# The state space model's input in DRAM: stored gapless and once, instead of with a repeated strip

## The chip, the cores and the metric

The kernel runs on 1 core of one Trainium2 chip. The metric is the device time of one execution in microseconds (us), median of several runs.

## What is computed

Two layers of a diffusion backbone over 768 tokens (256 context tokens, then 512 latent tokens), width 1024. In each layer four groups of heads share one input projection and one output projection: a complex diagonal state space model (S5), a Hyena long convolution, a retention, and a latent attention; then comes a gated feed-forward network. The change touches the S5 group alone:

```python
uc, ul = groups(u_ctx), groups(u_lat)
hc_f = s5_scan(uc, abar[0], bbar[0], None)
hc_b = s5_scan(uc[:, ::-1], abar[1], bbar[1], None)
hl_f = s5_scan(ul, abar[0], bbar[0], hc_f[:, -1])
hl_b = s5_scan(ul[:, ::-1], abar[1], bbar[1], hc_b[:, -1])
...
y = y.reshape(bsz, n, W_GROUP) + d_skip.astype(f32) * u.astype(f32)
y = jax.nn.gelu(y)
y = y * jax.nn.sigmoid(y @ glu_w.astype(f32) + glu_b.astype(f32))
```

The forward scan runs over context, then latent tokens. The backward scan runs over the context reversed, then over the latent tokens reversed; this is the same as reading the order "latent, context" from its end.

## The kernel before, in words

The input projection (L341 and L356, three fp32r passes a product) runs job after job on TensorE (PE). Weights come through `load_w` (L301: a DMA of 512 KB into one of three buffers `wr`; L305: a cast to `wh` on ScalarE (ACT); L306: the rest `wl` on VectorE (DVE)). Beside the projection jobs run generators, a few steps after each job: `chain_a` (S5 and retention), `chain_b` (attention, with its heads' scores at L1360 to L1362 and exponentials at L1420), `chain_h` (Hyena). In layer 0 retention comes before S5 in `chain_a`, in layer 1 S5 comes first. Each engine runs its instructions in one fixed order; an instruction that waits holds up all behind it on its engine.

The S5 group takes 8 neighbouring tokens as one chunk: NCH = 96 chunks, of which 32 are context and 64 latent. A channel's row is stored as [j = 8 tokens of a chunk][n = chunk].

- `s5_in` (L965 to L974) runs twice a layer, once for each 128 channels. ACT copies the projection from PSUM into a tile `t` [128, 8, 96] (L970, L971). Two DMAs on SP's queue store it into `s5_u`, whose rows are [8, 128]: L973 stores all 96 chunks of each j (runs of 384 bytes), L974 stores chunks 0 to 31 once more behind them, at 96 to 127 (runs of 128 bytes), so that a row reads context, latent, context.
- `s5_run` (from L976) turns the data: tile U (tag A_U) holds (j, channel in group) on the partitions and (group, chunk) along a row. For each j one DMA on POOL's software queue (L983) loads 16 partitions x 16 groups x 128 chunks: 256 runs of 512 bytes, 128 KB. Between them L984 loads the matching part of the matrix T (tag A_T), also 128 KB, 512-byte runs. `states` (L1001) multiplies U[.., 0:96] for the forward direction and U[.., 127:31:-1] for the backward one. `outputs` (L1033 to L1041) writes y, ACT's queue stores it to `s5_y` (L1050).
- At the end, the skip term d_skip * u needs u once more in its first layout: L1067 reads it from `s5_u` on SP's queue, as 8 runs of 384 bytes a channel in layer 0, and of 256 bytes (latent chunks alone) in layer 1. L1068 reads y, L1069 adds them on DVE, L1070 is the gelu.

Queues around the change: SP issues all weight loads and nearly all other transfers; POOL issues U, T and the four row copies of each pair of attention heads (L1371, L1373); ACT issues `s5_y`. POOL also computes the reciprocal roots of the norms (L404) and clears a column of the scan tiles (L1017).

Of the kernel before, what the change touches and what calls it, by code (L numbers as in the profile page):

```python
# [19 lines left out]
L = 2  # L20
# [7 lines left out]
NCH = NT // 8  # L28
# [197 lines left out]
def tile_kernel(ctx, tc, I, out, dbg=None, upto=None):  # L226
    nc = tc.nc
    act, dve, pe, pool, sp = nc.scalar, nc.vector, nc.tensor, nc.gpsimd, nc.sync
    qa, qs, qv, qb, qy, qh, qc, qm, qw, qp = [dict(s=sp, a=act, p=pool)[c] for c in QUEUES]
# [6 lines left out]
    def new(p, shape, tag, dt=F32, **kw):  # L236
        return p.tile(list(shape), dt, tag=tag, name=nm(tag), **kw)
# [22 lines left out]
    def st_tile(dt=F32):  # L260
        return new(wp, [128, NT], "st", dt, bufs=4)
# [167 lines left out]
    def dtile(shape, tag):  # L429
        return new(dr, shape, tag)  # L430
# [5 lines left out]
    s5_rot = [dtile([2, 4, 128, 576], f"s5_rot{l}") for l in range(L)]  # L436
    hy_K = [dtile([4, 2, 128, 768], f"hy_K{l}") for l in range(L)]
    hy_Kc = dtile([2, 2, 128, 768], "hy_Kc")
    s5_u = [dtile([256, 8, 128], f"s5_u{l}") for l in range(L)]
    s5_y = [dtile([256, 8, NCH], f"s5_y{l}") for l in range(L)]  # L440
    cat_d = [[dtile([128, NT], f"cat{l}_{i}") for i in range(8)] for l in range(L)]
    pd = [[dtile([128, NT], f"pd{l}_{i}") for i in range(19)] for l in range(L)]
# [522 lines left out]
    def s5_in(l, inproj):  # L965
        for i in range(2):
            o = inproj(i, (1, 0), True)
            t = st_tile().rearrange("p (j n) -> p j n", j=8)
            tv = t.rearrange("p j n -> p n j")
            act.copy(tv[:, 32:96], o[1].rearrange("p (n j) -> p n j", j=8))  # L970
            act.copy(tv[:, 0:32], o[0].rearrange("p (n j) -> p n j", j=8))  # L971
            u = s5_u[l][128 * i:128 * i + 128]
            qs.dma_start(u[:, :, 0:96], t)  # L973
            qs.dma_start(u[:, :, 96:128], t[:, :, 0:32])  # L974

    def s5_run(l, p, put, segs, busy=lambda: False):  # L976
        ud, yd = s5_u[l].rearrange("(g c) j n -> j c g n", c=16), s5_y[l].rearrange("(g c) j n -> j c g n", c=16)
        n0 = 0 if 0 in segs else 32
        nn = NCH - n0
        U = new(p, [128, 16, 128], "A_U")  # L980
        T = new(p, [128, 16, 128], "A_T")
        for j in range(8):
            qp.dma_start(U[16 * j:16 * j + 16], ud[j])  # L983
            qp.dma_start(T[16 * j:16 * j + 16].rearrange("c g (i x) -> c g i x", i=8), s5_T[l][:, :, j:j + 8, :])  # L984
        tt = dve.tensor_tensor

# [77 lines left out]
        for i in range(2):  # L1064
            tu = new(p, [128, 2, 8, NCH], ("A_U", "A_T")[i])
            t, u = tu[:, 0], tu[:, 1]
            qc.dma_start(u[:, :, n0:], s5_u[l][128 * i:128 * i + 128][:, :, n0:96])  # L1067
            qc.dma_start(t[:, :, n0:], s5_y[l][128 * i:128 * i + 128][:, :, n0:])  # L1068
            dve.scalar_tensor_tensor(t[:, :, n0:], u[:, :, n0:], vec256[:, l, 0, i:i + 1], t[:, :, n0:], ALU.mult, ALU.add)  # L1069
            act.activation(t[:, :, n0:], t[:, :, n0:], AF.Gelu_apprx_tanh)  # L1070
            yr.append(t)
            un.append(u.rearrange("p j n -> p (j n)"))
# [548 lines left out]
    for l in range(L):  # L1621
# [4 lines left out]
        def inproj(i, sg, fine=False):  # L1626
            if i in opened:
                return opened.pop(i).rest()
            return dense(blk(load_w(fl(I["w_in"][l, i]))), of(H), range(KD), sg, fine)
# [40 lines left out]
        with ExitStack() as base, ExitStack() as esl, ExitStack() as esr:  # L1670
# [5 lines left out]
            if l == 0:  # L1676
# [9 lines left out]
                with mkpool("start", side="right") as px:  # L1686
# [30 lines left out]
                    sp.dma_start(rr, I["k_rrope"])  # L1717
                    lgam = ret_gamma(px)
            s5_in(l, inproj)

            def ip_hyena(i):
# [52 lines left out]
            def chain_a(p):  # L1774
                for c in ORDER[l]:
                    if c == "s":
                        yield from s5_run(l, p, put, segs)
                    else:
                        while not (have("r") and have("g")):
                            yield  # L1780
                        yield from ret(l, p, put, segs)
                while spec or not have("h"):
                    yield
                if l == 0:
                    yield from hyena(l, p, put, 0, dict(v="A_U", x1=None, o="A_CA", y="A_SB", ny=2, kt="A_GT", u="A_HS", ri=None, pr=None))
# [73 lines left out]
        if True:  # L1859
# [47 lines left out]
            with mkpool("F") as p:  # L1907
# [38 lines left out]
                for gi, gn in enumerate(FFG):  # L1946
                    mid = []
                    for t in range(t0, t0 + gn):
                        uv = []
                        for w in range(2):  # L1950
                            run(g, W_FF)
                            o = product(("up", 2 * t + w), fl(I["w_up"][l, 2 * t + w]), H, segs)
                            u = st_tile()
# [65 lines left out]
def _build(nc, arrays, dbg=None, upto=None):  # L2019
    I = {k: nc.dram_tensor("in_" + k, v.shape, mybir.dt.from_np(v.dtype), kind="ExternalInput").ap() for k, v in arrays.items()}  # L2020
    out = nc.dram_tensor("out_x", [128, KD, NL], F32, kind="ExternalOutput").ap()
    with tile.TileContext(nc, schedule_with_timeline_sim=TLS) as tc:
        tile_kernel(tc, I, out, dbg, upto)
# [12 lines left out]
```

## Time and profile before

| | us |
|---|---|
| median of 3 runs | 2082.46 |
| lowest, highest | 2080.05, 2084.06 |
| the profiled execution, its own time | 2080.39 |
| its span, first to last instruction | 2078.6 |

The profile is of one execution. Times are us from the span's start. In a timeline row stand: start, duration, engine, line, operation, tile written and tile read, count, and in brackets the idle time before it with what ended it. A suffix q (SPq, ACTq) means the engine's sequencer, where DMAs are issued. In a row by windows stand: the stretch, its length, then for PE, PE's weight loads, DVE, ACT and POOL the busy time and (in brackets) the instructions, then the clock granted to PE (1.00 is 2.4 GHz, 0.50 is 1.2 GHz), the mean busy share of the 16 DMA engines (a little over 1 where packets of several queues overlap) and GB/s. In a row of waits stand: the engine and line that waited, for whom, us in total, times, longest. In a row of DMA queues stand: packets, MB, and the time of their packets as a share of 16 engines in that stretch; in one of DMA issues the transfer, the queue, the count, its size, and median us from issue to landing.

### The profile page before, as it was taken

How to read it: one execution, taken by the hardware profiler on the slowest of the kernel's cores; microseconds unless marked ns; L12 is line 12 of the kernel's file. 1: busy time of each engine (PE TensorE's matmuls, PEld its weight loads, DVE VectorE, ACT ScalarE, POOL GpSimd, SP SyncE). 2: the span in 40 equal slices, each digit the busy share in tenths (PEclk: the TensorE clock that was granted, in tenths of full speed). 3: DMA queues.
4: the chain of work that ended last, by engine and by line, in shares of the span. 5: the costliest groups of instructions: out<-in, count | busy, mean ns of one | idle time of the engine just before them, and what ended most of it. 6: DMA issues, size and time to landing. Idle time of an engine off the chain costs nothing. (4 is left out here: it accounts for less than half of the span.)

```text
span 2078.6 us, 29481 instructions
## 1 busy us (share of the span) xinstructions
PE 1912.3 (92%) x11318; PEld 1559.5 (75%) x11318; DVE 1299.4 (63%) x2444; ACT 788.0 (38%) x1349; POOL 172.3 (8%) x195
## 2 busy tenths in 40 slices
PE   5998999787899799899999999889989989999997
PEld 1866766566788688788888888778857878888885
DVE  4767553686735997776765444739857445555554
ACT  4546322343234433333533233433255434333332
POOL 0221013100001000110000000110022010000001
PEclk8999999889999899999999999999989989999998
DMA  8556556635442568234234222486631324333331
GB/s 299 178 182 227 168 177 172 147 78 175 148 152 92 172 216 276 78 115 140 63 98 149 68 65 67 119 215 184 217 98 53 133 85 128 93 100 94 99 99 44
DMA packets 147125, 283.94 MB, mean 137 GB/s; under 512 B 35397, under 2 KB 78566, under 8 KB 146984
## 3 DMA queue, kind: packets, MB, share of 16 engines
q1 hardware_dynamic: 139304, 273.65, 41.5%
q0 software_dynamic: 3072, 7.08, 1.9%
q10 hardware_dynamic: 4608, 1.31, 0.3%
q8 instruction: 90, 1.47, 0.3%
q14 instruction: 51, 0.42, 0.1%
HBM read 230.12 MB, written 48.99 MB: 134 GB/s over the span
## 5 line engine op out<-in xcount | busy, mean ns | idle before, releaser
L306 DVE TENSOR_TENSOR wl<-wr,wh 128x1024 fp32r<-128x1024 f32 x174 | 213.9, 1231 | 285.3 <-ACT wh L305 285.1
L341 PE MATMUL mm<-H1h,wh 128*128 128x512 f32 x888 | 355.6, 400 | 14.1 <-DVE st L426 13.1
L341 PE MATMUL mm<-H1h,wl 128*128 128x512 f32 x888 | 353.2, 398 | 0.3 <-DVE wl L306 0.3
L341 PE MATMUL mm<-H1l,wh 128*128 128x512 f32 x888 | 352.9, 397 | 0.0
L305 ACT CAST wh<-wr 128x1024 fp32r<-128x1024 f32 x174 | 182.1, 1050 | 356.7 <-PE mm L341 299.8
L341 PEld LDWEIGHTS mm<-H1h,wh 128*128 128x128 f32 x888 | 168.5, 190 | 55.3 <-issue 13.2
L341 PEld LDWEIGHTS mm<-H1l,wh 128*128 128x128 f32 x888 | 168.4, 190 | 38.8 <-issue 2.6
L341 PEld LDWEIGHTS mm<-H1h,wl 128*128 128x128 f32 x888 | 168.4, 190 | 37.8 <-issue 0.8
L341 PE MATMUL mm<-H0h,wh 128*128 128x256 f32 x480 | 137.0, 286 | 8.7 <-DVE st L426 8.5
L341 PE MATMUL mm<-ff_mh,wh 128*128 128x512 f32 (+1 forms) x432 | 134.9, 362 | 8.5 <-DVE y L1943 3.8
L341 PE MATMUL mm<-H0l,wh 128*128 128x256 f32 x480 | 137.5, 286 | 0.0
L341 PE MATMUL mm<-H0h,wl 128*128 128x256 f32 x480 | 137.4, 286 | 0.0
L341 PE MATMUL mm<-ff_ml,wh 128*128 128x512 f32 (+1 forms) x432 | 133.3, 359 | 0.0
L341 PE MATMUL mm<-ff_mh,wl 128*128 128x512 f32 (+1 forms) x432 | 132.7, 359 | 0.0
L404 POOL TENSOR_TENSOR rq_y<-rq_v,halves 128x2 f32<-128x2 f32 (+3 forms) x37 | 34.8, 942 | 1155.3 <-DVE rq_v L403 702.7
L341 PEld LDWEIGHTS mm<-H0h,wh 128*128 128x128 f32 x480 | 91.9, 191 | 12.8 <-issue 12.0
L341 PEld LDWEIGHTS mm<-H0l,wh 128*128 128x128 f32 x480 | 91.6, 191 | 5.3 <-issue 4.6
L341 PEld LDWEIGHTS mm<-H0h,wl 128*128 128x128 f32 x480 | 91.7, 191 | 4.0 <-issue 3.7
L341 PEld LDWEIGHTS mm<-ff_mh,wh 128*128 128x128 f32 x432 | 73.1, 191 | 24.0 <-DVE y L1943 5.3
L1943 DVE TENSOR_TENSOR y<-mm,y 128x512 f32<-128x512 f32 x80 | 53.4, 687 | 58.9 <-PE mm L341 58.8
L424 ACT ACTIVATE st<-mm,c_ffn_v 128x512 f32<-128x512 f32 (+1 forms) x132 | 88.3, 700 | 4.6 <-PE mm L356 4.6
L425 DVE SCALAR_TENSOR_TENSOR st<-mm,c_ffn_v,st 128x511 f32<-128x511 f32 (+1 forms) x132 | 83.4, 654 | 3.5 <-ACT st L424 3.5
(609 smaller groups left out, 4142.4 us busy)
## 6 DMA issues: line engine op xcount, KB each, us to landing
wr<-in_w_up SPq DMA_DIRECT2D x88, 512.0 KB, 3.6
ar<-in_ada_t SPq DMA_DIRECT2D x48, 512.0 KB, 4.4
wr<-in_w_down SPq DMA_DIRECT2D x44, 512.0 KB, 3.6
ar<-in_ada_w SPq DMA_DIRECT2D x40, 512.0 KB, 5.6
wr<-in_w_in SPq DMA_DIRECT2D x34, 512.0 KB, 5.7
ar<-in_k_tabl SPq DMA_DIRECT2D x16, 512.0 KB, 4.2
wr<-in_w_out SPq DMA_DIRECT2D x16, 512.0 KB, 4.9
xs_d<-x SPq DMA_DIRECT2D x8, 1024.0 KB, 4.7
```

The source lines that it names most:

```text
L305: act.copy(hi, raw)
L306: dve.tensor_tensor(lo, raw, hi.bitcast(F32), ALU.subtract)
L341: pe.matmul(outs[s], w, X(k, s, j), start=f, stop=z)
L404: pool.tensor_tensor(y, v, halves[:, :n], ALU.pow)
L424: act.activation(u[:, o:o + m], ps, AF.Identity, bias=vw[:, 3:4], scale=vw[:, 1:2])
L425: dve.scalar_tensor_tensor(u[:, o + 1:o + m], ps[:, 0:m - 1], vw[:, 0:1], u[:, o + 1:o + m], ALU.mult, ALU.add)
L1943: dve.tensor_tensor(d, ps, d, ALU.add)
```

## The change

`s5_u` gets rows of [8, 96], gapless. `s5_in` stores each tile with one DMA, whose runs are whole rows (8 x 96 x 4 = 3072 bytes). U is loaded by two DMAs for each j: chunks 0 to 95 (runs of 384 bytes) into columns 0 to 95, and chunks 0 to 31 once more (runs of 128 bytes, 32 KB) into columns 96 to 127. The skip term's read takes whole rows, in layer 1 the context chunks too. Instructions of a layer: SP issues 2 DMAs fewer, POOL 8 more.

```diff
-    s5_u = [dtile([256, 8, 128], f"s5_u{l}") for l in range(L)]
+    s5_u = [dtile([256, 8, NCH], f"s5_u{l}") for l in range(L)]
...
-            u = s5_u[l][128 * i:128 * i + 128]
-            qs.dma_start(u[:, :, 0:96], t)
-            qs.dma_start(u[:, :, 96:128], t[:, :, 0:32])
+            qs.dma_start(s5_u[l][128 * i:128 * i + 128], t)
...
-            qp.dma_start(U[16 * j:16 * j + 16], ud[j])
+            qp.dma_start(U[16 * j:16 * j + 16, :, 0:NCH], ud[j])
+            qp.dma_start(U[16 * j:16 * j + 16, :, NCH:128], ud[j][:, :, 0:128 - NCH])
             qp.dma_start(T[16 * j:16 * j + 16].rearrange("c g (i x) -> c g i x", i=8), s5_T[l][:, :, j:j + 8, :])
...
-            qc.dma_start(u[:, :, n0:], s5_u[l][128 * i:128 * i + 128][:, :, n0:96])
+            qc.dma_start(u, s5_u[l][128 * i:128 * i + 128])
```

## Rows read from the trace of the kernel before

**Rows 1.** The page's first part, busy time.
```profile
PE 1912.3 (92%) x11318; PEld 1559.5 (75%) x11318; DVE 1299.4 (63%) x2444; ACT 788.0 (38%) x1349; POOL 172.3 (8%) x195
```

**Rows 2.** Windows around S5's loads, layer 0 (375 on), layer 1 (1390 on).
```profile
375.00:380.00 5.00, 1.56 (x6) 0.97 (x6) 2.57 (x5) 0.84 (x3) 3.69 (x7) 0.76 1.14 224
380.00:385.00 5.00, 3.53 (x10) 2.98 (x11) 1.03 (x2) 0.93 (x2) 1.81 (x5) 0.50 1.05 124
...
1390.00:1400.00 10.00, 10.00 (x46) 8.68 (x46) 3.21 (x4) 4.34 (x8) 0.00 (x0) 0.76 0.67 222
```

**Rows 3.** Waits of PE, stretch 340 to 420 (first) and 1340 to 1400.
```profile
PE mm L1360 <- DMA B_Q<-st: 5.7, 2, 3.8
...
PE mm L341 <- DVE st L426: 8.5, 1, 8.5
```

**Rows 4.** Timeline of ACT, layer 1.
```profile
1385.78 1.04 ACT L305 CAST wh<-wr 128x1024 fp32r<-128x1024 f32 x1 [11.00 <-DMA wr<-in_w_v]
1386.73 0.77 ACT L424 ACTIVATE st<-mm,c_hy_v 128x512 f32<-128x512 f32 x1
```

**Rows 5.** Timeline of SP's DMA issues, layer 1.
```profile
1349.75 5.43 SPq L989 DMA_DIRECT2D A_SB<-s_SB  x1
...
1357.09 2.50 SPq L301 DMA_DIRECT2D wr<-in_w_in  x1
...
1367.96 0.99 SPq L301 DMA_DIRECT2D wr<-in_w_v  x2
```

**Rows 6.** Timeline of POOL, layer 1.
```profile
1362.25 1.12 POOL L983 DMA_DIRECT2D A_U<-s_u  x2 [16.16 <-DMA s_u<-st]
...
1370.43 0.56 POOL L984 DMA_DIRECT2D A_T<-s_T  x1 [3.75 <-DMA A_U<-s_u]
```

**Rows 7.** DMA queues, 1364 to 1388: the software queue and its landings.
```profile
q0 software_dynamic: 528, 1.44, 35.8%
...
wr<-in_w_v SPq DMA_DIRECT2D x2, 512.0 KB, 17.7
A_U<-s_u POOLq DMA_DIRECT2D x5, 128.0 KB, 13.0
```

**Rows 8.** Windows: the first store of s5_u (layer 0), and large runs alone (layer 1).
```profile
72.00:73.00 1.00, 1.00 (x10) 1.00 (x10) 1.00 (x2) 0.85 (x1) 0.00 (x0) 1.00 0.92 253
73.00:74.00 1.00, 1.00 (x11) 1.00 (x10) 0.90 (x5) 0.98 (x2) 0.00 (x0) 1.00 1.22 258
74.00:75.00 1.00, 1.00 (x11) 1.00 (x10) 0.38 (x3) 0.90 (x3) 0.00 (x0) 1.00 0.48 54
...
1386.00:1388.00 2.00, 0.00 (x0) 0.00 (x0) 1.14 (x1) 1.51 (x2) 0.00 (x0) 0.50 1.02 396
```

**Rows 9.** DMA queues, 333 to 348, layer 0: three loads of U alone.
```profile
q0 software_dynamic: 144, 0.39, 10.8%
```

**Rows 10.** Timeline of POOL, layer 0.
```profile
333.24 1.71 POOL L983 DMA_DIRECT2D A_U<-s_u  x3 [6.45 <-ACT A_gw L1201]
...
354.74 2.24 POOL L984 DMA_DIRECT2D A_T<-s_T  x4 [2.93 <-DVE A_CA L1220]
...
381.61 0.56 POOL L984 DMA_DIRECT2D A_T<-s_T  x1 [2.91 <-DMA B_Q<-st]
```

**Rows 11.** Timeline, layer 0, ACT and PE; layer 1's first states.
```profile
389.25 0.62 ACT L397 CAST H1h<-st 128x512 fp32r<-128x512 f32 x1 [2.06 <-DMA st<-cat]
...
393.55 1.40 PE L1001 MATMUL sm<-A_U,A_SB 128*64 128x96 f32 x16
...
1405.66 1.54 PE L1001 MATMUL sm<-A_U,A_SB 128*64 128x96 f32 x32
```

**Rows 12.** DMA issues 484 to 492 (the skip term's reads), and DVE's wait.
```profile
A_U<-s_u SPq DMA_DIRECT2D x1, 384.0 KB, 3.8
A_U<-s_y SPq DMA_DIRECT2D x1, 384.0 KB, 4.2
...
506.66 1.02 DVE L1069 SCALAR_TENSOR_TENSOR A_T<-A_T,c_vec 128x768 f32<-128x768 f32 x1 [1.95 <-DMA A_T<-s_y]
```

## The prediction, made before the change was run

> **What bounds the kernel now.** The page first: PE is busy 1912.3 of 2078.6 us [rows 1], so at most some 166 us of its time are idle, and a change of transfers can only win or lose what PE waits for them. So I looked for idle PE next to the changed transfers, by windows and by PE's waits. There are two places. In layer 0, from 375 on, PE works 1.56 and 3.53 of two stretches of 5 us, and the DMA engines are full (share 1.14, 1.05) [rows 2]; its largest wait there is 5.7 us for the row copies of the attention heads [rows 3]. In layer 1, shortly after 1380, PE stands still for 8.5 us [rows 3]; afterwards it runs a while at 1.2 GHz, so the next 10 us have a mean clock of 0.76, about 2.4 us more [rows 2]. The row names DVE's last convolution step, but that step stood behind ACT: ACT waited 11.00 us for a weight of the retention (w_v), and only then evicted the projection [rows 4]. That weight was issued at 1367.96 and took 17.7 us to land [rows 5, 7]. Layer 1's stall is therefore a DMA queue that is full, and S5's stores and loads are part of what fills it.
>
> Everything else about the change is hidden. DVE's wait for the skip term in layer 0 is for y, not for u [rows 12], and the first states of layer 1 come at 1405.66, 35 us after POOL's last transfer but two, and U takes 13.0 us to land [rows 6, 7, 11].
>
> **The store, two a layer.** Two transfers (384 KB in 384-byte runs, 128 KB in 128-byte runs) become one of 384 KB in 3072-byte runs. Before, one pair keeps the engines busy for 0.92 + 1.22 + 0.48 = 2.6 us [rows 8]. Large runs move 396 GB/s [rows 8], so 393 KB take 1.0 us. Saved: 1.6 us a pair, 3.2 us a layer. In layer 0 PE is busy throughout that stretch [rows 8], so it is worth nothing there; if that cover were gone, 1.6 us a pair. One issue on SP goes with each pair, and SP is not a bound. In layer 1 the stores lie right before the issues at 1349.75 and 1357.09, in front of the weight, in the full stretch: 3.2 us count. They also jam SP: those two issues took 5.43 and 2.50 us, where the two of the weight took 0.99 together [rows 5].
>
> **U's loads, 8 more a layer on POOL.** Each 128 KB load (256 runs of 512 bytes, so 16 runs an engine) becomes one of 96 KB and one of 32 KB, twice the runs for the same bytes. Price of one load now: 10.8% of 15 us for 3 loads is 0.54 us of all engines, alone [rows 9]; 35.8% of 24 us for 1.44 MB (11 loads of U and T) is 0.78 us in the full stretch [rows 7]. No row shows the split load, so two bounds: priced by bytes it adds nothing; priced by runs it adds as much again, 8 x 0.54 to 8 x 0.78 = 4.3 to 6.2 us a layer. I take a value between, from the same rows: at 396 GB/s over 16 engines a 512-byte run needs 21 ns for its bytes, and takes 34 ns (0.54 us / 16) to 49 ns (0.78 / 16); the 13 to 28 ns above that are the price of a run. 128 more runs an engine: 1.7 to 3.6 us, so 2.6 us a layer.
>
> What the row shows of short runs on SP's queue is milder: u in 384-byte runs landed in 3.8 us, y of the same size in whole rows in 4.2, issued just behind it [rows 12]. The Trainium skill ("DMA: Bandwidth & Descriptors", Specifications) says that transfers under 512 bytes miss line rate because the engine reads, modifies and writes; by it the old runs of 512 just pass and both new ones fail. Rows 12 do not show it for 384 bytes; no run here shows it for 128 bytes on the software queue. By that rule the sum would be rival 1's, below.
>
> **Layer 1, sum.** The engines are full until the weight lands, so work taken from in front of it counts one for one, whoever's it is: -3.2 + 2.6 = -0.6 us. Bounds: -3.2 (bytes) to +3.0 (runs). The loads of U start when the store has landed, at 1362.25 [rows 6]; with the store's end some 3 to 4 us earlier they start earlier, but against the same weights. I count -0.6. The loads must wait in turn: at 1370.43 POOL waits 3.75 us for an earlier load of U to land, eight transfers before it [rows 6]; that is the number POOL keeps in flight. With 19 instead of 11 to issue there (five of T have gone before), the last goes out near 1380; what stands behind it on POOL is a clearing of the scan tiles needed after 1405 [rows 11], so the wait is covered by 20 us.
>
> **Layer 0, sum.** POOL's loads begin at 333.24, as soon as retention frees the buffer, and are spread: 3, then 2 more before 354, then 4 of T from 354.74, and, behind the attention's row copies, 3 of U and 4 of T up to 381.61 [rows 10]. If the 16 new loads take the same places, 5 go early and 11 come behind the row copies, together 15 instead of 7, where DMA is full [rows 2]. POOL's last load already waits 2.91 us for the eighth transfer before it, a row copy [rows 10]. Each further one waits for the landing of one issued about 8 us earlier, so the last leaves near 389 and lands at 393 to 396. The first states stand at 393.55 on PE [rows 11], which goes in order: 0 to 2.5 us late. The same extra work (5.5 pairs of about 1.1 us, instead of 3 loads of 0.78: +3.8 us) also pushes the reads that ACT waits for at 389.25, 2.06 us, before the exponentials that PE needs [rows 11]. Bounds: 0, if the short loads go out in the idle time of POOL behind 357 [rows 10], to +6 by runs. I take +2, near the lane arithmetic. What is late next is the attention scores behind the states on PE.
>
> **The skip read.** Two a layer: 1024 runs become 128; in layer 1 it reads 384 KB instead of 256. The first reads land before DVE asks for them; by the pair of landings, 3.8 and 4.2 us [rows 12], there is nothing to win: 0, bounds -0.5 to +0.5, hidden by the wait for y.
>
> **Total.** +2 - 0.6 + 0 = +1.4 us. The profiled execution took 2080.4 us (span 2078.6, 1.8 around it), so 2081.8 in its terms; it lies 2.1 under the median of the runs shown, and in the median's terms I say 2083.9.
>
> **Rivals.**
> 1. Slower: the run is the price, not the byte. Each 128-byte run costs what a 512-byte one does: layer 0 up to +6, layer 1 up to +3.0, so +5 to +9 us, 2087 to 2091. It decides from the point where the split pair takes over about 1.2 us of the engines. For it: loads of 1.44 MB hold 35.8% of the engines in a stretch that moves little, and U takes 13.0 us to land [rows 7]. Against it: 34 ns a run when alone [rows 9]. The skill's rule on 512 bytes would make this outcome. Chance 0.31.
> 2. Faster: SP's queue is freed. SP is stuck for about 5 and 2 us behind the short runs of the stores [rows 5]. If both go, the weights behind them are issued 3 to 5 us sooner, casts and stores follow, and the weight that ACT waits for lands up to 5 us sooner; a stall cut from 8.5 to 3.5 us may also spare the 2.4 us at the low clock. With layer 0 at its bound of 0 that is up to -7.4, with the skip read at its own -0.5 about -8, at best 2074; with layer 0 at +2 and the clock not won it is -3 and still inside "same". Against it: the engines are full anyway, so an earlier issue only queues earlier. Chance 0.26.
> 3. The change doesn't do what it says: the store still moves 384-byte runs. Then layer 1 loses the 3.2 us less the short strip's share (about 2), for +2 to +4 in all; but y's gapless rows are read the same way and land as fast [rows 12]. Chance 0.03, inside "same".
>
> **Numbers.** About 0.2% (4 us) is what a measurement of this kernel can tell from no change. The forecast, -4 to +4 us, has 0.40; with rival 3 "same" has 0.43, faster 0.26, slower 0.31. The range takes rivals 1 and 2 to their ends, 2074 to 2091. The likeliest case's own is 2080 to 2086.
>
> **What would show it.** Right: in layer 1 no SP issue over 1 us behind the store; POOL's first load of U near 1358 instead of 1362; the stall near 1381 within 2 us of 8.5; in layer 0 the last load of U issued near 389 and a short wait of PE on it. Rival 1: the software queue's share from 1364 to 1388 well above 35.8% for the same MB, U landing after 13 us or more, the stall over 10 us. Rival 2: the weight landing near 1381, the stall under 5 us. Wrong altogether: a different order of instructions on PE or POOL that moves other stages by more than these sums.

## The result and the profile after

The changed kernel is slower: 2104.76 us (2103.86 to 2110.78) where the kernel before, beside it, takes 2081.26. The ratio is 1.0108, with a 95% interval of 1.0090 to 1.0126. A second comparison, in another set of runs, gave 2097.12 against 2083.20, a ratio of 1.0072 (1.0047 to 1.0098). The forecast was 2083.9, range 2074 to 2091. Both medians lie above the range.

The page of the changed kernel, first part:

```profile
PE 1926.5 (92%) x11318; PEld 1569.1 (75%) x11318; DVE 1296.9 (62%) x2444; ACT 791.7 (38%) x1351; POOL 182.7 (9%) x211
```

Against [rows 1], PE does the same 11318 matmuls and is busy 14.2 us longer. The span is 23.9 us longer, so some 10 us of the loss are idle time of PE; the rest is the same matmuls taking longer, at a mean granted clock of 0.948 where it was 0.955. The page does not say where. The two traces laid side by side do: for each line of PE's matmuls the k-th one of after was set against the k-th one of before, and the median shift was read near some times of before. It is +2.5 us at 363, +2.8 at 546, +4.6 at 1356, +2.3 at 1400, and +22.7 from 1637 to the end. So a few us are gone by layer 1, 2.5 of them already at 363, ahead of layer 0's states; layer 1's stall gives a little back, and **20.4 us go between 1400 and 1637 of before**. The prediction had no term for that stretch.

**Layer 0.** The last load of U on POOL, the first states on PE, and PE's waits from 340 to 420, after:

```profile
389.26 0.56 POOL L982 DMA_DIRECT2D A_U<-s_u  x1 [0.22 <-issue]
...
397.46 1.55 PE L1000 MATMUL sm<-A_U,A_SB 128*64 128x96 f32 x16 [2.60 <-DMA A_U<-s_u]
```
```profile
PE mm L1359 <- DMA B_Q<-st: 4.3, 2, 3.4
...
PE sm L1000 <- DMA A_U<-s_u: 2.6, 1, 2.6
```

This is the predicted wait, in place and size: the last load of U is issued at 389, and PE waits 2.6 us for it, where before no wait stood [rows 11]. The row copies' wait went from 5.7 to 4.3 [rows 3]. Little of this stays: the shift is +2.5 us ahead of the wait (363) and +2.8 behind it (546).

**Layer 1, transfers.** SP's issues, POOL's loads of U, and the software queue from 1364 to 1388, after:

```profile
1346.56 0.33 SPq L988 DMA_DIRECT2D A_SB<-s_SB  x1
...
1353.05 0.32 SPq L972 DMA_DIRECT2D s_u<-st  x1
...
1355.01 0.38 SPq L301 DMA_DIRECT2D wr<-in_w_in  x1
...
1357.73 0.32 SPq L972 DMA_DIRECT2D s_u<-st  x1
...
1366.13 2.55 SPq L301 DMA_DIRECT2D wr<-in_w_v  x2
```
```profile
1362.64 0.56 POOL L981 DMA_DIRECT2D A_U<-s_u  x1 [13.65 <-DMA s_u<-st]
...
1369.28 0.56 POOL L981 DMA_DIRECT2D A_U<-s_u  x1 [2.19 <-DMA A_U<-s_u]
...
1380.59 0.56 POOL L982 DMA_DIRECT2D A_U<-s_u  x1 [1.45 <-DMA A_T<-s_T]
```
```profile
q0 software_dynamic: 820, 1.55, 39.8%
...
A_U<-s_u POOLq DMA_DIRECT2D x7, 96.0 KB, 8.0
...
A_U<-s_u POOLq DMA_DIRECT2D x7, 32.0 KB, 8.3
```

SP's two stuck issues are gone: 0.33 and 0.38 us stand where 5.43 and 2.50 stood [rows 5]. The two of w_v took 2.55 us, though, where they took 0.99, so the sign "no SP issue over 1 us" is not met. The one store landed after 2.5 us (median of four), where the two of a pair landed after 4.6 and 5.4, so the store is the cheaper one that was forecast. POOL's first load of U starts at 1362.64. With the shift of 4.6 us at that place, that is 1358.0 of before's time, 4 us sooner, as forecast. The queue holds the engines 9.55 us (39.8% of 24) for 1.55 MB in 820 packets, where it held them 8.6 us for 1.44 MB in 528 [rows 7], so the shorter runs are hardly dearer. The last load of U leaves POOL at 1380.59, which is 1376.0 in before's time, no later than forecast.

PE's waits from 1340 to 1400, after:

```profile
PE mm L341 <- DVE st L426: 5.7, 1, 5.7
```

The stall shrank from 8.5 to 5.7 us [rows 3], by more than the 2 us that the prediction's sign allowed.

**Layer 1, the states.** The first and the last states, and the last matmul of the dense projection (L341), after:

```profile
1431.78 0.88 PE L1000 MATMUL sm<-A_U,A_SB 128*64 128x96 f32 x16
...
1483.88 0.88 PE L1000 MATMUL sm<-A_U,A_SB 128*64 128x96 f32 x16
...
1496.25 0.39 PE L341 MATMUL mm<-H1h,wl 128*128 128x512 f32 x1
```

The last states and the last matmul of the dense projection, before:

```profile
1455.18 0.88 PE L1001 MATMUL sm<-A_U,A_SB 128*64 128x96 f32 x16
...
1526.01 0.39 PE L341 MATMUL mm<-H1h,wl 128*128 128x512 f32 x1
```

The states come at 1431.78 instead of 1405.66 [rows 11], and their row shows no wait. U's last load had been issued 51 us earlier. They are late because 153 other matmuls now stand ahead of them **in PE's instruction list**. That order is fixed when the program is built: in the list of before layer 1's first states are matmul number 6744, in the list of after number 6897. (A list has 9916 matmuls; some of them, the states among them, leave two records each, which makes the 11318 of the page.) The two lists differ in two places only, from matmul 284 to 1516 (start-up and layer 0) and from 6744 to 7349 (this one). The edit touches no line of PE's work; how the builder came to the new order is not shown here. The dense work that moved ahead of the states is then missing behind them. Before, it ran on for 71 us after the last states began (1455 to 1526); now it does so for 12 us (1484 to 1496).

Windows (columns as in [rows 2]), before and then after, and after that PE's largest waits from 1480 to 1567 of the changed kernel:

```profile
1400.00:1480.00 80.00, 77.75 (x562) 68.40 (x562) 72.77 (x162) 24.48 (x43) 0.63 (x6) 1.00 0.59 185
1480.00:1520.00 40.00, 38.75 (x214) 33.44 (x213) 23.73 (x50) 17.97 (x32) 1.75 (x3) 1.00 0.69 207
1520.00:1560.00 40.00, 32.03 (x166) 22.30 (x168) 24.62 (x57) 19.80 (x47) 11.74 (x15) 0.83 0.26 71
```
```profile
1400.00:1480.00 80.00, 80.00 (x574) 71.04 (x573) 53.56 (x114) 24.27 (x42) 0.63 (x6) 1.00 0.49 159
1480.00:1520.00 40.00, 34.80 (x172) 28.59 (x170) 31.43 (x75) 7.31 (x13) 0.00 (x0) 0.96 0.64 209
1520.00:1560.00 40.00, 28.35 (x99) 20.19 (x100) 19.83 (x32) 18.18 (x36) 11.95 (x16) 0.70 0.28 80
```
```profile
PE sm L882 <- issue: 3.5, 1, 3.5
PE sm L419 <- POOL rq_y L404: 3.3, 2, 1.8
PE sm L413 <- ACT B_R L1296: 2.9, 1, 2.9
PE sm L959 <- DVE h_v L918: 2.4, 1, 2.4
PE sm L1084 <- ACT A_T L1069: 1.8, 1, 1.8
```

Up to 1480 PE is full, fuller than before; DVE, which runs the scan, falls from 72.77 to 53.56 us. From 1480 to 1560 PE then stands idle for 16.9 of 80 us where it was 9.2. The mean granted clock from 1520 on is 0.70 instead of 0.83, so TensorE spends more of the stretch at the lower of its levels, 1.2 GHz. The waits are a handful of 2 to 4 us each, between steps of the chains (convolution, norms, attention, the gate of the state space model); the 3.5 us named "issue" wait for nothing that the profile shows. None is for a transfer of the change.

The whole tail in one window, the same work by the shifts, before and then after:

```profile
1400.00:1637.00 237.00, 220.56 (x1519) 182.95 (x1519) 176.96 (x401) 106.25 (x224) 28.37 (x40) 0.95 0.44 137
```
```profile
1402.30:1659.70 257.40, 230.10 (x1519) 190.24 (x1518) 179.29 (x401) 104.26 (x222) 27.96 (x40) 0.91 0.40 127
```

Of the 20.4 us, 10.9 are idle time of PE (16.4 before, 27.3 after). The other 9.5 are the same 1519 records taking longer, where the mean granted clock is 0.91 instead of 0.95. So nearly half of the tail is not idle time, but work at 1.2 GHz.

### The profile page after: what moved, and what is told of

Its sections match the earlier page's. It is cut to its first block, busy times and chain, and to the rows that moved or that the text cites. A ratio compares the mean times of both kernels' runs of the same rounds, so it can differ in the third digit from the quotient of the medians.

```text
span 2102.5 us, 29504 instructions
## 1 busy us (share of the span) xinstructions
PE 1926.5 (92%) x11318; PEld 1569.1 (75%) x11318; DVE 1296.9 (62%) x2444; ACT 791.7 (38%) x1351; POOL 182.7 (9%) x211
## 5 line engine op out<-in xcount | busy, mean ns | idle before, releaser
L341 PE MATMUL mm<-H1h,wh 128*128 128x512 f32 x888 | 356.5, 401 | 14.5 <-DVE st L426 13.5
L341 PE MATMUL mm<-H1h,wl 128*128 128x512 f32 x888 | 353.3, 398 | 0.3 <-DVE wl L306 0.3
L341 PE MATMUL mm<-H1l,wh 128*128 128x512 f32 x888 | 352.6, 397 | 0.0
L341 PEld LDWEIGHTS mm<-H1h,wh 128*128 128x128 f32 x888 | 168.9, 190 | 56.5 <-issue 14.6
L341 PEld LDWEIGHTS mm<-H1l,wh 128*128 128x128 f32 x888 | 168.8, 190 | 38.4 <-issue 2.4
L341 PEld LDWEIGHTS mm<-H1h,wl 128*128 128x128 f32 x888 | 168.7, 190 | 37.7 <-issue 0.8
L341 PE MATMUL mm<-H0h,wh 128*128 128x256 f32 x480 | 137.4, 286 | 5.9 <-DVE st L426 5.7
L341 PE MATMUL mm<-ff_mh,wh 128*128 128x512 f32 (+1 forms) x432 | 133.6, 360 | 9.7 <-DVE y L1942 5.2
L341 PE MATMUL mm<-H0h,wl 128*128 128x256 f32 x480 | 138.3, 288 | 0.0
L341 PE MATMUL mm<-H0l,wh 128*128 128x256 f32 x480 | 137.4, 286 | 0.0
L341 PE MATMUL mm<-ff_mh,wl 128*128 128x512 f32 (+1 forms) x432 | 132.5, 358 | 0.0
L341 PE MATMUL mm<-ff_ml,wh 128*128 128x512 f32 (+1 forms) x432 | 132.4, 357 | 0.0
L341 PEld LDWEIGHTS mm<-H0h,wh 128*128 128x128 f32 x480 | 92.1, 192 | 12.5 <-ACT st L1730 6.0
L341 PEld LDWEIGHTS mm<-H0l,wh 128*128 128x128 f32 x480 | 91.8, 191 | 6.2 <-issue 5.8
L341 PEld LDWEIGHTS mm<-H0h,wl 128*128 128x128 f32 x480 | 92.1, 192 | 3.8 <-issue 3.4
L341 PEld LDWEIGHTS mm<-ff_mh,wh 128*128 128x128 f32 x432 | 72.6, 190 | 25.6 <-DVE y L1942 6.6
```

Source lines behind the costliest of these rows:

```text
L341: pe.matmul(outs[s], w, X(k, s, j), start=f, stop=z)
```

## The experiments

Main theory, "order": the time goes by where layer 1's state space model stands in PE's fixed list. Rival, "transfers": the short runs, the longer queue or the new store and read cost time on the chip. The expectations up to u_first_before count eight matmuls more, to the end of the first eight states (6752 before, 6905 after); those after that give the places used here (6744, 6897).

The readings of all kernels in one table. "First states" is the place of layer 1's first states in PE's list, "last dense" that of the last projection matmul, both counted from 1; before has 6744 and 7294. "Stall" is the shift from 1356 to 1400 of before and "tail" that from 1400 to 1637, both in us, by the method above, from each kernel's profiled execution.

| kernel | first states | last dense | stall | tail | ratio to before (95%) |
|---|---|---|---|---|---|
| changed | 6897 | 7206 | -2.3 | +20.4 | 1.0108 (1.0090 to 1.0126) |
| after_again | 6897 | 7206 | -9.0 | +20.1 | 1.0072 (1.0047 to 1.0098) |
| only1 | 6897 | 7206 | -8.0 | +19.4 | 1.0069 (1.0044 to 1.0094) |
| split | 6897 | 7206 | -4.6 | +19.1 | 1.0056 (1.0036 to 1.0077) |
| tiny_l1 | 6901 | 7206 | -10.9 | +18.8 | 1.0058 (1.0041 to 1.0075) |
| split7_l1 | 6889 | 7206 | -3.7 | +17.5 | 1.0048 (1.0030 to 1.0066) |
| split6_l1 | 6875 | 7250 | -7.4 | +6.5 | 1.0003 (0.9986 to 1.0020) |
| tiny3_l1 | 6875 | 7250 | -10.2 | +14.6 | 1.0002 (0.9988 to 1.0017) |
| tiny2_l1 | 6849 | 7250 | -10.9 | +10.7 | 0.9980 (0.9961 to 0.9998) |
| split4_l1 | 6847 | 7250 | -0.2 | +4.4 | 1.0003 (0.9986 to 1.0019) |
| copy_dve | 6847 | 7250 | -5.8 | +3.3 | 0.9982 (0.9964 to 1.0000) |
| split2_l1 | 6797 | 7266 | -1.1 | +2.4 | 1.0008 (0.9993 to 1.0023) |
| t_to_act_l1_after | 6761 | 7294 | -10.4 | +1.5 | 0.9961 (0.9945 to 0.9978) |
| t_to_act_both_after | 6761 | 7294 | -10.9 | -1.3 | 0.9960 (0.9945 to 0.9976) |
| only0 | 6744 | 7294 | -0.6 | +3.8 | 1.0008 (0.9992 to 1.0023) |
| t_to_sp_after | 6704 | 7294 | +2.9 | +5.2 | 1.0010 (0.9994 to 1.0026) |
| u_first_before | 6693 | 7294 | together | +7.9 | 1.0029 (1.0014 to 1.0044) |
| copy_dve_t_to_act_l1 | 6678 | 7294 | together | -3.5 | 0.9943 (0.9925 to 0.9961) |
| t_to_act_l1_before | 6613 | 7294 | together | +11.2 | 1.0050 (1.0033 to 1.0068) |

In the last two and in u_first_before the order already differs before 1400, so their two stretches stand together. The tails are of one execution each, and not always a typical one: that of split7_l1 took 2102.13 us, the longest of ten, that of after_again 2092.22, the shortest of five. The ratios are of all runs.

### One layer, one part

```diff
 # only0, only1: rows of [8, 96], the one store, the split loads and the whole-row read for l == 0 (or l == 1) alone
-    s5_u = [dtile([256, 8, 128], f"s5_u{l}") for l in range(L)]
+    s5_u = [dtile([256, 8, NCH if l == 0 else 128], f"s5_u{l}") for l in range(L)]
```

> The change in layer 0 alone (gapless rows, split loads, whole-row skip read there; layer 1 as before). Theory 'order': the loss comes from layer 1, where the state space model's first states stand later in the fixed order of PE's instructions; layer 0's order is the same as before, so only the few us of its late loads are lost: 2082 to 2086 us, layer 1's first states at 1405 to 1411. Rival 'transfers': the short runs and the eight more loads on POOL's queue cost time on the chip in either layer; the 22 us fall in about equal parts: 2090 to 2095.

> The change in layer 1 alone. Theory 'order': layer 1 has 46 us of other matmuls ahead of its first states in PE's fixed order that stood behind them before; 2097 to 2103 us, first states at 1428 to 1433 though U has landed some 40 us earlier. Rival 'transfers': 2090 to 2095, and PE shows a wait for U.

```diff
 # split: the kernel before, with only this
-            qp.dma_start(U[16 * j:16 * j + 16], ud[j])
+            qp.dma_start(U[16 * j:16 * j + 16, :, 0:NCH], ud[j][:, :, 0:NCH])
+            qp.dma_start(U[16 * j:16 * j + 16, :, NCH:128], ud[j][:, :, NCH:128])
```

> The old layout, stores and skip read; only U is loaded by two transfers for each j (columns 0 to 95 and 96 to 127, both from the wide rows). PE's instructions then stand in the same order as in the changed kernel. Theory 'order': as slow as the changed kernel, 2101 to 2108, first states near 1432. Rival 'store and skip read': the loss comes from the gapless store or the whole-row read, and the split alone stays within 5 us of before, 2080 to 2086.

Measured: only0 2083.18 us, only1 2097.18, split 2096.03, against 2083.15 for the kernel before. Layer 0 alone cannot be told from no change; its own wait is there. Against the expectation its list in layer 0 is not that of before: it differs from matmul 284 to 1516, as the changed kernel's does. PE's waits from 340 to 420 in only0:

```profile
PE sm L1008 <- DMA A_U<-s_u: 3.3, 1, 3.3
```

Layer 1 alone gives all of the loss that after_again shows. Its size is at the lower end of what was expected, and its first states come at 1422.3, not at 1428 to 1433, since the stall came out 8 us shorter. The split alone, with the old store and the old read, gives the same as the whole of layer 1. It is 5 us short of its expected range, but its tail is that of the changed kernel. So the gapless store and the whole-row read are not needed for the loss.

### The same order without the transfers, the same transfers without the order

```diff
 # t_to_sp_after: the changed kernel, with T on SP's queue
-            qp.dma_start(T[16 * j:16 * j + 16]...
+            qs.dma_start(T[16 * j:16 * j + 16]...
 # t_to_act_l1_after and t_to_act_l1_before: on ACT's queue, in layer 1
+            (qy if l else qp).dma_start(T[16 * j:16 * j + 16]...
 # tiny_l1: the kernel before, and behind each load of U
+            for _ in range(4 if l else 0):
+                qp.dma_start(U[16 * j:16 * j + 1, 0:1, 0:16], ud[j][0:1, 0:1, 0:16])
```

> The changed kernel once more, on the same chip as the three beside it. Layer 0 alone gave a ratio of 1.0008 and layer 1 alone 1.0069; if the two parts simply add, 1.006 to 1.010 here, that is about 2095 to 2104 us where before takes 2083. If they work on each other, it lies above 1.010 again, as in the first comparison (1.0108).

> The kernel before, with four added transfers of 64 bytes behind each of U's eight loads in layer 1 (32 in all, 2 KB; they load once more what the load before them brought). Layout, stores, U's loads and the skip read are those of before. PE's first states of layer 1 then have 6909 matmuls ahead of them (changed kernel 6905, before 6752). Theory 'order': no short run carries anything, and yet 2091 to 2099 us, as with the real split. Rival 'transfers': 2 KB cost nothing, 2081 to 2086.

> The changed kernel with T's loads moved from POOL's queue to SP's; all 16 split loads of U remain on POOL. In PE's fixed order the first states of layer 1 then stand about where they stood before (6712 matmuls ahead of them; before 6752, changed 6905). Theory 'order': 2079 to 2086, first states at 1395 to 1410. Rival 'transfers': the short runs are still there, and eight loads more stand on SP's queue, so 2098 to 2108.

> The changed kernel, with T's eight loads of layer 1 on ACT's DMA queue in place of POOL's. All short runs, the 16 split loads on POOL, the gapless store and the whole-row read stay. PE's first states of layer 1 have 6769 matmuls ahead of them, nearly as before. Theory 'order': layer 1's loss is gone and layer 0's few us are left: 2081 to 2088, first states of layer 1 at 1400 to 1412, and SP's queue is not held up as it was with T there. Rival 'transfers': 2095 to 2104.

> The kernel before, with T's eight loads of layer 1 on ACT's queue. PE's first states of layer 1 have only 6621 matmuls ahead of them, 131 fewer than before. Theory 'order': the sooner the state space model ends, the less of its tail is exposed behind the projections; if the tail of before was still exposed, 2070 to 2079 us. Rival 'U is not there yet': the order now puts the states at a place where U has not landed on the chip; PE waits 5 to 15 us for it near 1375 and the time is 2080 to 2092.

Measured: after_again 2097.12 us, tiny_l1 2095.37, t_to_act_l1_after 2077.05, t_to_act_l1_before 2093.00, with 2083.20 for the kernel before; t_to_sp_after 2085.60 with 2083.15. tiny_l1 carries 2 KB more than before and loses nearly what layer 1 alone loses (1.0058 against 1.0069). Its POOL and PE, layer 1:

```profile
1362.56 1.13 POOL L983 DMA_DIRECT2D A_U<-s_u  x2 [15.96 <-DMA s_u<-st]
...
1419.03 0.49 POOL L985 DMA_DIRECT2D A_U<-s_u  x1 [1.79 <-DMA A_U<-s_u]
...
1421.45 1.54 PE L1003 MATMUL sm<-A_U,A_SB 128*64 128x96 f32 x32 [0.47 <-issue]
```

The tiny transfers do hold up POOL's queue, to 1419, but PE waits only 0.47 us there. t_to_act_l1_after is the reverse: it has every short run, all 16 loads of U on POOL, the new store and read, and an order close to that of before; T's loads on another queue are what brings that order. It is faster than both kernels, and than expected (2081 to 2088). Its first states, and the weight's cast on ACT:

```profile
1381.15 1.05 ACT L305 CAST wh<-wr 128x1024 fp32r<-128x1024 f32 x1 [2.70 <-DMA wr<-in_w_v]
...
1404.84 0.88 PE L1000 MATMUL sm<-A_U,A_SB 128*64 128x96 f32 x16
```

ACT waits 2.70 us for the weight instead of 11.00 [rows 4], and PE's stall there is 0.3 us. So the rival "transfers" falls in both directions.

The two others show what an early order meets. In t_to_sp_after the six loads of T on SP stand ahead of the weights, and PE waits 11.5 us for a weight. SP's issues and PE's wait:

```profile
1353.33 3.82 SPq L983 DMA_DIRECT2D A_T<-s_T  x6
```
```profile
PE mm L341 <- ACT wh L305: 11.9, 2, 11.5
```

In t_to_act_l1_before the states stand 131 matmuls sooner, and PE waits there; its 2093.00 us lie 1 us above the range of that theory. The place was as expected, but what came last was not U: it was the matrix SB on SP's queue. PE's waits from 1360 to 1400:

```profile
PE sm L1001 <- DMA A_SB<-s_SB: 4.2, 1, 4.2
PE sm L1033 <- issue: 1.9, 1, 1.9
```

### A miss, and the question behind it

```diff
 # copy_dve: the changed kernel
-            qp.dma_start(U[16 * j:16 * j + 16, :, NCH:128], ud[j][:, :, 0:128 - NCH])
...
+        dve.tensor_copy(U[:, :, NCH:128], U[:, :, 0:128 - NCH])
 # copy_dve_t_to_act_l1: the same, with T on ACT's queue in layer 1
 # u_first_before: the kernel before, T's loads in a loop of their own behind U's
 # t_to_act_both_after: the changed kernel, T on ACT's queue in both layers
```

> The changed kernel with the repeated strip filled on the chip: U is loaded by one transfer for each j (96 chunks), and one copy on DVE writes columns 96 to 127 from columns 0 to 31. No transfer is added against before. PE's first states of layer 1 have 6855 matmuls ahead of them (before 6752, changed 6905), since the copy stands behind all eight loads. Theory 'order': still slower than before, 2089 to 2098. Rival 'eight more transfers on POOL': that cost is gone and the gapless store's gain is left, 2076 to 2084.

> As copy_dve, with T's eight loads of layer 1 on ACT's queue: 6686 matmuls ahead of layer 1's first states, 66 fewer than before. If the place of the states alone decides and U lands in time (its last load leaves POOL some 5 us after the store), 2070 to 2079. If this place is already too early for U, PE waits for it and it is 2080 to 2092, as with 6621 matmuls ahead (2093.0).

> The kernel before, with all eight loads of U issued ahead of the eight of T, in both layers, still on POOL. 6701 matmuls ahead of layer 1's first states, 51 fewer than before. If U lands in time: 2074 to 2082. If PE has to wait, for U or later for T, which now lands last: 2083 to 2092.

> The changed kernel with T's loads on ACT's queue in layer 0 too. Layer 1's order is that of the kernel with T moved in layer 1 alone (2077.05). If layer 0 loses time because POOL's last loads of U wait their turn behind other transfers (forecast: the last one issued near 389), 16 loads instead of 24 end sooner, layer 0's first states come at 390 to 394 instead of 398, and the time is 2071 to 2076. If ACT's queue has to wait for the buffer and holds up what ACT does behind it, 2078 to 2088.

Measured, with 2082.34 for the kernel before: copy_dve 2080.68 us, copy_dve_t_to_act_l1 2071.42, u_first_before 2088.26, t_to_act_both_after 2075.04. copy_dve missed: its states stand two thirds of the way to those of the changed kernel, and its tail cost 3.3 us instead of some 13. So the place of the states alone is not the measure. The time lies in the range of its rival, eight more transfers on POOL (2076 to 2084). That rival falls with tiny2_l1 and tiny3_l1 below, which have 16 and 24 more transfers there than before and lose nothing (0.9980 and 1.0002). u_first_before lost, though its states stand sooner and PE waited for neither U nor T. Its stall was 9.0 us, and the 7.9 us from 1356 on are not explained. t_to_act_both_after lies in its range, but not for the reason given: its first states of layer 0 came at 398.7, not at 390 to 394. Their wait for U is gone (its last load leaves POOL at 384.84), but they stand behind attention scores, which wait themselves. copy_dve_t_to_act_l1 is the fastest of all. There PE hardly waits at the early place, since the copy is ready in time:

```profile
1380.48 0.88 PE L1000 MATMUL sm<-A_U,A_SB 128*64 128x96 f32 x16 [0.15 <-DVE A_U L983]
```

What else differs is the place of the last dense matmul: 7250 in copy_dve, 7206 in the changed kernel. Two edits vary the two places apart: fewer tiny transfers, and a split of only the first 2, 4, 6 or 7 of the eight loads.

```diff
 # split2_l1 to split7_l1: the kernel before (here with six)
+            if l and j in (0, 1, 2, 3, 4, 5):
+                qp.dma_start(U[16 * j:16 * j + 16, :, 0:NCH], ud[j][:, :, 0:NCH])
+                qp.dma_start(U[16 * j:16 * j + 16, :, NCH:128], ud[j][:, :, NCH:128])
+            else:
                 qp.dma_start(U[16 * j:16 * j + 16], ud[j])
```

> The kernel before, with two added transfers of 64 bytes behind each of U's loads in layer 1 (16 in place of the 32 of tiny_l1). 6849 matmuls stand ahead of layer 1's first states (tiny_l1 6901, copy_dve 6847, before 6744), and the last matmul of the dense projection is number 7250 of PE's order, as in copy_dve (before 7294; tiny_l1 and the changed kernel 7206). Theory 'filler': what costs is that dense matmuls are used up ahead of the state space model and are missing beside its tail and the retention; while some 7250 stand, little is lost: from 1400 to 1637 of before some +3 us as in copy_dve (+3.3), and with the stall of layer 1 shorter by 5 to 10, 2073 to 2082 us. Theory 'place': the loss grows in proportion to the place of the first states, 105 of 157 positions of tiny_l1's +19 us: +13, 2083 to 2092.

> The same with three added transfers of 64 bytes a load (24). 6875 matmuls stand ahead of layer 1's first states, 131 more than before, but the last matmul of the dense projection is number 7250, as with two. Theory 'filler': +3 us from 1400 to 1637 of before, 2073 to 2082 us. Theory 'place': 131 of 157 of +19, that is +16, 2086 to 2095.

> The kernel before, with only the first two of U's eight loads split, in layer 1 alone. 6797 matmuls stand ahead of layer 1's first states (before 6744, all eight split 6897) and the last dense matmul is number 7266 (before 7294, all eight split 7206). Measured from 1400 to 1637 of before, where all eight split lost 19 to 20 us: theory 'place' 53 of 153 of that, +7; theory 'filler' +1 to +3.

> The first four loads split. First states behind 6847 matmuls, last dense matmul number 7250: the places of copy_dve, with four added transfers and the old stores. Theory 'place' +13 from 1400 to 1637 of before; theory 'filler' +3, as copy_dve.

> The first six loads split. First states behind 6875 matmuls, last dense matmul still number 7250. Theory 'place' +16 to +17 from 1400 to 1637 of before; theory 'filler' +3. U's loads are issued early here, so the wait for U on the chip that blurred tiny2_l1 and tiny3_l1 should be missing.

> The first seven loads split, one more than in the run beside it. First states behind 6889 matmuls (14 more), last dense matmul number 7206 (44 sooner, one job of the projection). Theory 'place' +18 from 1400 to 1637 of before, hardly more than with six; theory 'filler' +19, a jump of some 16 us against six.

Measured: tiny2_l1 2081.43 us and tiny3_l1 2085.29 (before 2084.14); split2_l1 2086.68, split4_l1 2086.87, split6_l1 2083.84 and split7_l1 2093.25 (before 2083.95). The two tiny kernels settled nothing between place and filler: in them PE waited for U on the chip (4.13 and 3.40 us at the first states), and their tails lie between the theories. The splits decide more. From two to six split loads the tail grows by about 2 us for each two, and the ratio stays at 1.000 to 1.001. **The seventh adds 11 us to the tail and takes the ratio to 1.0048**; the medians of ten runs each lie 9.4 us apart. The seventh moved the states by 14 places and the last dense matmul by 44. The first states and the last dense matmul, split6_l1 and then split7_l1:

```profile
1421.52 1.54 PE L1005 MATMUL sm<-A_U,A_SB 128*64 128x96 f32 x32
...
1512.38 0.39 PE L341 MATMUL mm<-H1h,wl 128*128 128x512 f32 x1
```
```profile
1431.68 1.54 PE L1005 MATMUL sm<-A_U,A_SB 128*64 128x96 f32 x32
...
1498.16 0.39 PE L341 MATMUL mm<-H1h,wl 128*128 128x512 f32 x1
```

PE's list from matmul 7180 on shows what that does (D dense projection, s states, o outputs, g gate of the state space model, h convolution, - attention, norms and retention):

```
before     DDDDDDDDDDDDDDDDDDDDDDhgghDDhhhhhhDDDggggggDDDDDDDDDDD------DD------DDDDDDD-DDDDDDDDDDDD-------DD--------DDDDDDDDDD---
split6_l1  DDDDDDDDDhhhhhhhhDDhhhhoooooooooooohhhhhhhhhhhhhhhhDhhhhDDDDDDDDDDDDDDDhgghhhhhhhgggggg-------------------------------
split7_l1  DhhhhDDDDDDDDDDDDDDDDDDDDDDhhhhhhhhhhhhoooooooooooohhhhhhhhhhhhhhhhhhhhhgghhhhgghhhgggg-------------------------------
changed    DDDDDDDDDhhhhDDDDDDDDDDDDDDhhhhhhhhhhhhoooooooooooohhhhhhhhhhhhhhhhhhhhhgghhhhgghhhgggg-------------------------------
```

In split6_l1, 16 dense matmuls still stand between the model's last outputs and its gate, the place where y is stored, read back and passed through the gelu. In split7_l1 and in the changed kernel no dense matmul stands behind the last outputs. Before, dense work filled every gap down to the attention. Windows from the last outputs to the gate, and then of the whole tail, first split6_l1 and then split7_l1:

```profile
1500.20:1512.70 12.50, 12.50 (x57) 10.44 (x57) 8.83 (x21) 4.84 (x7) 0.00 (x0) 1.00 0.83 221
...
1396.70:1640.20 243.50, 221.60 (x1517) 184.64 (x1518) 181.75 (x405) 109.35 (x230) 28.53 (x40) 0.94 0.44 140
```
```profile
1508.90:1520.60 11.70, 9.06 (x41) 7.33 (x40) 8.04 (x18) 4.04 (x6) 0.00 (x0) 1.00 0.81 217
...
1403.70:1658.20 254.50, 229.53 (x1519) 189.79 (x1519) 181.44 (x404) 104.99 (x224) 28.02 (x40) 0.91 0.42 132
```

Up to the gate PE is never idle in split6_l1, and for 2.6 us in split7_l1. Over the whole tail idle time grows by 3.1 us (21.9 to 25.0), and busy time by 7.9 us, at a mean clock of 0.91 instead of 0.94. So in these two executions most of the step is work at 1.2 GHz beside a few more short waits, not the waits themselves. The ten runs of each point the same way: the mean granted clock of a whole execution is 0.955 in split6_l1 and 0.952 in split7_l1.

## Why the prediction was wrong

**The step that failed** is in the sum of layer 1. It took POOL's longer run of issues, "the last goes out near 1380", against states "needed after 1405", and concluded that "the wait is covered by 20 us". The first half held (1380.59). The second took 1405.66, a time of the old trace, as if it belonged to the states. It belonged to their place in PE's list, and the list was built anew: eight more loads ahead of the states put 153 more matmuls ahead of them. No wait for U came of it; what the sum left out is the order itself, a term put at nothing without a reason. The prediction named this outcome only as what would make it "wrong altogether", without a price and a chance. The price is the tail: 17.5 to 20.4 us in the six kernels with the last dense matmul at 7206, whatever their transfers. In the changed kernel 10.9 us of it are idle PE and 9.5 us work at the lower clock.

**Layer 0, +2 us: the wait right, the time not shown.** The last load left at 389 and PE waited 2.6 us (3.3 in only0). Layer 0 alone measured a ratio of 1.0008, that is +1.7 us (-1.7 to +4.8), which fits +2 and can't be told from nothing. The wait itself may cost less: the shift grows by 0.3 us across it in the changed kernel, and t_to_act_both_after, which is without it, has the ratio of t_to_act_l1_after, which has it (0.9960, 0.9961).

**Layer 1's transfers, -0.6 us: right in sign, too small.** From 1356 to 1400 the changed kernel won 2.3 us, and 9.0 in its second profile. Rival 2's prize, a stall cut to 3.5 us or less, is real: in t_to_act_l1_after it is 0.3. Its cause is not only SP's queue, as the rival had it: tiny_l1 keeps the old stores and shows no wait for that line there. Its loads of U leave POOL later, which would make room for the weight; that is argued, not shown. Why the same kernel wins 2.3 us in one profile and 9.0 in another, where its stall is 1.8 us, stays open. This difference, and that at 1356 (+4.6 against -0.6), is what separates the two profiles; the tails agree.

**The price of a run: between the bounds, near the lower.** Rival 1 fell. The queue held the engines 1 us longer, not 4 to 6, and t_to_act_l1_after, with all short runs, is faster than before. The rule that transfers under 512 bytes miss line rate, from the Trainium skill ("DMA: Bandwidth & Descriptors", Specifications), would have made the new runs dear. What may show of it here is that 32 KB in 128-byte runs land no sooner (8.3 us) than 96 KB in 384-byte runs (8.0); no run shows that it costs an engine time in layer 1.

**The skip read, 0: right.** DVE's wait before the skip term is still for y:

```profile
510.00 1.02 DVE L1068 SCALAR_TENSOR_TENSOR A_T<-A_T,c_vec 128x768 f32<-128x768 f32 x1 [2.35 <-DMA A_T<-s_y]
```

**Shown and not shown.** Shown: the order costs the tail without the split loads (tiny_l1), the split loads without the order cost nothing (t_to_act_l1_after), and the loss has a step where the last dense matmul moves from 7250 to 7206 (split6_l1 to split7_l1), most of it, in the profiled executions, at the lower clock. Argued from the lists and waits alone: that the step comes from the dense work missing between the outputs and the gate, where only 2.6 us of new idle time lie. The two places never moved apart entirely, and some 2 us for each two split loads, the tail of tiny3_l1 (its list is that of split6_l1 but for two matmuls, its tail 8 us longer and its ratio the same) and the loss of u_first_before are left over.

## What to carry to other kernels

Where the instruction order of an engine is fixed when the program is built, an edit to a few transfers can move work that no transfer waits for: compare the built lists of both programs before pricing anything, and don't use a time of the old trace as a deadline for the new one. Ask of a chain that slips not only whether it is late, but what is left to run beside its end: here, as more loads were split, the tail stayed within 7 us until the filler behind the chain's last outputs was used up, and then jumped by 11. And price the clock with the waits: of that jump 3 us were idle time and 8 the lower clock. The remedy was not in the transfers that were changed: moving eight others (T) off the same queue gave the place back and made the kernel with gapless rows faster than before; with the strip copied on DVE it is the fastest, 2071.42 us, a ratio of 0.9943 (0.9925 to 0.9961).

## What was not expected of the hardware

Loads of 32 KB and of 96 KB, with the same number of runs, landed after the same 8 us on the software queue, so in this stretch the bytes did not set the landing. And a transfer of 64 bytes landed about as late as one of 128 KB. The landings of both in tiny_l1, from 1364 to 1388:

```profile
A_U<-s_u POOLq DMA_DIRECT2D x3, 128.0 KB, 5.2
A_U<-s_u POOLq DMA_DIRECT2D x7, 0.1 KB, 5.0
```

The 32 of them drew out POOL's issues from the 20 us of the changed kernel to 56 us (1362.56 to 1419.03), because each writes the 64 bytes that the transfer before it wrote and waits for that one to land. POOL's first wait there is 7.50 us with two transfers under way, while in the changed kernel eight go out without a wait.
